# Recurrence of a hybrid encoder layer: filler in two runs per step, output one step later, x replaced in place

## The chip, the cores and the metric
One core of one Trainium2 chip. The metric is the device time of the whole kernel in microseconds, median of several runs. The engines are TensorE (PE, with its weight loads PEld), VectorE (DVE), ScalarE (ACT), GpSimd (POOL) and SyncE (SP); SP and POOL issue the DMAs of the part that matters here.

## What is computed
One encoder layer on a sequence of 2048 tokens of width 1024. A combined input projection feeds two mixers and two gates; this change touches the RWKV-7 mixer's delta-rule recurrence and the projection that runs beside it.
```
proj = x @ w_in                       # 43 columns of 128: hyena, rwkv, gates
def rwkv_step(S, inp):
    r, w, k, v, kk, a = inp
    sa = einsum('dbhvk,dbhk->dbhv', S, -kk)
    S = S * w[..., None, :] + sa[..., :, None] * (kk * a)[..., None, :] + v[..., :, None] * k[..., None, :]
    y = einsum('dbhvk,dbhk->dbhv', S, r)
    return S, y
_, ys = scan(rwkv_step, S0, xs)       # one scan per direction, then summed, normalized and gated
```
Behind it stand the hyena mixer's long convolutions by Fourier transform, the merge with the gates, and a SwiGLU feed-forward block.

## The kernel before
The program runs `project` (a part of the input projection and the recurrence's inputs), then `chain` (the recurrence), `hyena`, `merge` and `ffn`. The scan is done in chunks of 64 tokens: 32 chunks forward, then 32 backward, 64 steps (n = 0 to 63) in eight groups of eight. In `chain` the order on PE is written out by hand; the other engines' order is made by a scheduler from the program's order, priorities and its own times.

A step (`step(n)`, line 789) is three small products that hang on each other. **R** (tile pR, line 800) is the group's gram blocks G times the state and values in tile VS; ScalarE copies it (line 803). **S** (pS, line 808) applies the inverse X to that copy; ScalarE copies the result into tile SV (line 811). **D** (pD, line 816) is the state's update, which VectorE adds and scales into the next step's VS (lines 822, 823). The output **Y** (pY, lines 827 and 829) takes A, VS, SV and the masked gram Gr; in the backward half `normed` normalizes it on VectorE and ScalarE. All these products use part of the array (64 rows or columns); each is 8 calls, shown as 16 instructions.

Beside a step stands other work, `beside(n)`: **T**, the transposes pT of the next step's inputs (line 782); in steps 0 to 2 of a group three, three and two **grams** pG of the group that follows (line 677; rows ABp come by DMA into two buffers, VectorE masks the products, lines 656); in step 7 and the next group's step 0 the two halves of an **inverse** (`finish`, pW, lines 722 and 735). What `finish` needs is made by `invert`, issued after step 2: POOL moves the grams through DRAM (lines 696, 697), VectorE runs 62 small operations (lines 702, 704), transposes (line 709), and POOL stores (line 710). In the backward half there are also transposes pgt (line 865) and products pgg (line 897) of the output's gate. The PSUM tag "pg" has three buffers for all of these.

**Filler** is the rest of the input projection: 88 blocks of 128 columns by 512 tokens, each eight triples of passes (lines 202 to 204: hi by hi, lo by hi, hi by lo) over the whole array. `columns()` (line 908) yields a triple at a time. `order` goes through the four blocks of 512 tokens of x; one block lies on chip as xh and xl, so x is replaced three times. `share(n)` gives a step so much filler that filler and other work are even over the steps; in step 61 and after there is none.

`step` yields three times: after R, after S, and after D with Y. Each time `fill` gives a third of the filler and of the other work, in turns in proportion. Before a new x block `columns()` yields -14.0, and `hold` then keeps the filler back until steps of that cost have gone by:
```
def main():
    while True:
        t = next(more, None) if hold[0] <= 0 else None
        if t is None:
            return
        if t < 0:
            hold[0] = -t
            return
```
Of the kernel before, what the change touches and what calls it, by code (L numbers as in the profile page):

```python
# [9 lines left out]
F32 = mybir.dt.float32  # L10
# [6 lines left out]
P = 128  # L17
# [172 lines left out]
class Layer:  # L190
# [431 lines left out]
    def chain(self):  # L622
        tc, nc, i = self.tc, self.nc, self.i
        mm, tt, ts = nc.tensor.matmul, nc.vector.tensor_tensor, nc.vector.tensor_scalar
        NG, N = 8, 2 * NCH
        with tc.tile_pool(name="ch", bufs=1, reuse_waits="tile") as s, tc.tile_pool(name="chp", bufs=1, space=PSUM, reuse_waits="tile") as ps:
# [162 lines left out]
            def step(n):  # L789
# [3 lines left out]
                BK, SV = ins.pop(n)  # L793
                A = As[n % 2]
                VS = VSs.pop(n)
# [6 lines left out]
                with tc.high_priority(offset=AHEAD):  # L802
                    nc.scalar.copy(R, p)
                yield 0.33
                p = ps.tile([P, HP, 64], F32, name="pS", tag="pc", bufs=1)
# [3 lines left out]
                with tc.high_priority(offset=AHEAD):  # L809
                    for j in range(2):  # L810
                        nc.scalar.copy(SV[opp[j], j], p[opp[j]])
                yield 0.33
                pd = ps.tile([P, HP, 64], F32, name="pD", tag="pD", bufs=1)
# [3 lines left out]
                for j in range(2):  # L817
                    if (n + 1) % NCH == 0:
                        break
                    S1, q = VSs[n + 1][opp[j], j], opp[j]  # L820
                    with tc.high_priority(offset=AHEAD):
                        tt(out=S1, in0=pd[q], in1=VS[q, j], op=ALU.add)
                        tt(out=S1, in0=S1, in1=Dks[q, d, :, c:c + 1].broadcast_to([64, HP, 64]), op=ALU.mult)
                Y = ps.tile([P, HP, 64], F32, name="pY", tag="pY", bufs=1)
                for hp in range(HP):
# [8 lines left out]
                else:  # L834
                    normed(c, Y)
                yield 0.34

            out, ys = {}, {}

# [61 lines left out]

            xs = {2: self.x2}
            self.cut, self.rush, self.stores = 2, RUSH, nc.sync

            uh, gates = [*range(12)], [*range(27, NIN)]
            order = [(b, gates if b > 1 else uh + gates) for b in (2, 1, 3, 0)]

            def columns():
                seq = [(b, ct) for b, cts in order for ct in cts]
                nxt, raw = self.nxt  # L910
                for n, (b, ct) in enumerate(seq):
                    w = nxt
                    if n + 1 < len(seq):
                        nxt = self.parts(raw)
                    if b not in xs:
                        xs[b] = self.load_x(self.xp1, b, 1)
                    if n + 2 < len(seq):
                        raw = self.column(seq[n + 2][1])
                    if n and b != seq[n - 1][0]:
                        yield -14.0  # L920
                    yield from self.block(ct, b, *w, xs)

# [37 lines left out]

            hold = [0.0]

            def main():
                while True:
                    t = next(more, None) if hold[0] <= 0 else None
                    if t is None:
                        return
                    if t < 0:
                        hold[0] = -t
                        return  # L970
                    left[0] -= t
                    yield t


            def fill(need, aux, cost):
                d, a = main(), 0.0
                did = 0.0
                while did < need or a < cost:
# [14 lines left out]
                    else:  # L993
                        a += t

            with tc.manual_schedule(engines={mybir.EngineType.PE}):
                begin(0)
# [12 lines left out]
                near(0)  # L1010
                outward(0)
                self.fps = ps, "pg", 3
                taps, pieces = iter(()), [1, 2, 3]
                self.rush = 0
                for n in range(N):
                    g, st = divmod(n, NG)
                    if st == 0 and g + 1 < N // NG:
                        begin(g + 1)
                    cost, aux = beside(n)
                    sh = share(n)  # L1020
                    if n == LAST + 1:
                        taps = self.filt(0, 0)
                    if n >= LAST + 1:
                        aux.append(self.part(taps, 4.0))
                        cost += 4.0
                    if n + 1 < N:
                        outward(n + 1)
                    if n + 2 < N:
                        fetch(n + 2)
                    if n > NCH + 2 and n % 2 == 1:  # L1030
                        given(place(n - 2)[1])
                    for k in range(n + 1, N if n >= LAST else min(n + 2, N)):
                        if k not in VSs:
                            near(k)
                    if n == LAST:
                        self.open()
                    for need in step(n):
                        fill(sh * need, aux, cost * need)
                        hold[0] -= max((sh + cost) * need, 2.0)
                    fill(0.0, aux, 1e9)  # L1040
                    if n >= LAST and pieces:
                        self.taken(pieces.pop(0))
                    if st == len(GRAMS) - 1 and g + 1 < N // NG:
                        invert(g + 1)
                for part in (gated(2), channel_major(1), channel_major(0), gated(0)):
                    self.pull(part, 1e9)
                    self.pull(taps, 0.8)
# [633 lines left out]
```

## Time and profile before
| | us |
|---|---|
| median of 3 timed runs | 4077.75 (4075.48 to 4081.51) |
| the profiled execution | 4068.93 |
| its span in the profile | 4067.2 |
| from the first R to the R of step 61 | 875.1 |
| TensorE busy in these | 816.95 |

A row of time has the start, the duration, engine, line, operation, what is written and read, how many are merged, and in brackets the idle time before it with what ended it. Ends of products are modelled, so distances between starts tell what they take.

### The profile page before, as it was taken

The page shows a single profiled execution, that of the slowest core. Times are in us where ns is not written, and L with a number is a line of the kernel's source. Part 1 is how long each engine was busy: PE and PEld are TensorE (multiplying, and loading weights), DVE is VectorE, ACT ScalarE, POOL GpSimd, SP SyncE. Part 2 cuts the span into 40 slices and gives each one's busy share as a digit, 9 for nine tenths or more (in the row PEclk, how much of TensorE's full clock was granted, in tenths as well). Part 3 has the DMA queues.
Part 4 walks back from the last instruction along what each step waited for, and adds up shares of the span by engine and source line. Part 5 has one row for each costly group of instructions (what it writes and reads, how often), then busy time and mean ns, then how long its engine had stood idle before and what let it go on. Part 6 is the DMA issues. An engine that isn't in the chain of part 4 may idle for free. (4 is left out here: it accounts for less than half of the span.)

```text
span 4067.2 us, 64483 instructions
## 1 busy us (share of the span) xinstructions
PE 3870.1 (95%) x25872; PEld 3130.6 (77%) x25872; DVE 2421.1 (60%) x3823; ACT 1484.1 (36%) x2912; POOL 76.8 (2%) x107
## 2 busy tenths in 40 slices
PE   8999999899998999888898999999999999999998
PEld 6766557677776777788887899788888878888887
DVE  5456885556656666778877656544444465444444
ACT  3345662223335556756554323211111141111113
POOL 0000000000000000000000000000000000000000
PEclk9999999899898999899999999999999999999999
DMA  4556877666666766412224433411111133111111
GB/s 137 175 168 176 224 205 236 192 195 184 201 205 193 205 198 192 118 50 70 63 74 135 159 114 123 160 58 52 47 47 47 47 104 104 47 47 47 47 47 42
DMA packets 389186, 501.83 MB, mean 123 GB/s; under 512 B 134852, under 2 KB 270541, under 8 KB 388181
## 3 DMA queue, kind: packets, MB, share of 16 engines
q1 hardware_dynamic: 362775, 443.13, 36.3%
q10 hardware_dynamic: 20736, 37.80, 3.1%
q0 software_dynamic: 5376, 16.78, 1.5%
q8 instruction: 204, 3.34, 0.3%
q14 instruction: 95, 0.78, 0.1%
HBM read 352.74 MB, written 127.93 MB: 118 GB/s over the span
## 5 line engine op out<-in xcount | busy, mean ns | idle before, releaser
L202 PE MATMUL acc<-xh,wh 128*128 128x512 f32 x1376 | 606.4, 441 | 9.1 <-ACT xh L197 9.1
L203 PE MATMUL acc<-xl,wh 128*128 128x512 f32 x1376 | 551.9, 401 | 6.4 <-DVE xl L198 6.4
L204 PE MATMUL acc<-xh,wl 128*128 128x512 f32 x1376 | 551.0, 400 | 0.5 <-DVE wl L198 0.5
L1618 DVE TENSOR_TENSOR acc<-pd,acc 128x1024 f32<-128x1024 f32 x320 | 387.7, 1221 | 69.9 <-PE pd L204 64.2
L197 ACT CAST fwh<-raw 128x1024 fp32r<-128x1024 f32 x132 | 138.6, 1050 | 704.7 <-PE pg L203 487.9
L202 PEld LDWEIGHTS acc<-xh,wh 128*128 128x128 f32 x1376 | 262.3, 191 | 127.4 <-issue 46.9
L1646 DVE TENSOR_TENSOR h<-pu,sg 128x512 f32<-128x512 f32 x88 | 60.9, 692 | 493.1 <-PE pu L204 485.7
L204 PEld LDWEIGHTS acc<-xh,wl 128*128 128x128 f32 x1376 | 262.8, 191 | 63.9 <-DVE wl L198 1.0
L203 PEld LDWEIGHTS acc<-xl,wh 128*128 128x128 f32 x1376 | 264.5, 192 | 57.4 <-DVE xl L198 10.2
L198 DVE TENSOR_TENSOR wl<-wraw,wh 128x512 fp32r<-128x512 f32 (+1 forms) x217 | 170.3, 792 | 188.4 <-ACT wh L197 181.2
L202 PE MATMUL pd<-fwh,hh 128*128 128x512 f32 x704 | 276.1, 392 | 2.3 <-DVE acc L1616 1.9
L204 PE MATMUL pu<-fxh,fwl 128*128 128x512 f32 x704 | 277.8, 395 | 0.0
L204 PE MATMUL pg<-fxh,fwl 128*128 128x512 f32 x704 | 277.8, 395 | 0.0
L202 PE MATMUL pg<-fxh,fwh 128*128 128x512 f32 x704 | 276.7, 393 | 0.2 <-DVE fxl L1533 0.2
L203 PE MATMUL pg<-fxl,fwh 128*128 128x512 f32 x704 | 276.8, 393 | 0.0
L203 PE MATMUL pu<-fxl,fwh 128*128 128x512 f32 x704 | 276.4, 393 | 0.0
L202 PE MATMUL pu<-fxh,fwh 128*128 128x512 f32 x704 | 275.9, 392 | 0.4 <-ACT fxh L1532 0.4
L203 PE MATMUL pd<-fwl,hh 128*128 128x512 f32 x704 | 275.6, 391 | 0.0
L204 PE MATMUL pd<-fwh,hl 128*128 128x512 f32 x704 | 274.6, 390 | 0.0
L198 DVE TENSOR_TENSOR fwl<-raw,fwh 128x1024 fp32r<-128x1024 f32 x132 | 161.3, 1222 | 166.6 <-ACT fwh L197 162.6
L197 ACT CAST wh<-wraw 128x512 fp32r<-128x512 f32 (+1 forms) x217 | 151.1, 705 | 198.3 <-PE acc L203 182.0
L1187 DVE STREAM_TRANSPOSE V<-U 128x1024 f32<-128x1024 f32 x96 | 181.1, 1955 | 34.3 <-ACT U L1222 14.1
(299 smaller groups left out, 7617.1 us busy)
## 6 DMA issues: line engine op xcount, KB each, us to landing
wraw<-in_w_in SPq DMA_DIRECT2D x130, 512.0 KB
ABp<-ABd SPq DMA_DIRECT2D x64, 512.0 KB
raw<-in_fg SPq DMA_DIRECT2D x44, 512.0 KB
raw<-in_fu SPq DMA_DIRECT2D x44, 512.0 KB
raw<-in_fd SPq DMA_DIRECT2D x44, 512.0 KB
ud<-ev ACTq DMA_DIRECT2D x84, 256.0 KB
ABd<-AB SPq DMA_DIRECT2D x32, 512.0 KB
gated<-ev SPq DMA_DIRECT2D x64, 256.0 KB
```

The source lines that it names most:

```text
L197: nc.scalar.copy(hi, src)
L198: nc.vector.tensor_tensor(out=lo, in0=src, in1=hi.bitcast(F32), op=ALU.subtract)
L202: mm(ps, ah, bh, start=start, stop=False)
L203: mm(ps, ah, bl, start=False, stop=False)
L204: mm(ps, al, bh, start=False, stop=stop)
L1187: self.nc.vector.transpose(V[:, :, sl].rearrange("p j c -> p c j"), U[:, :, sl].rearrange("p n c -> p c n"))
L1618: tt(out=acc[t], in0=pf, in1=acc[t], op=ALU.add)
L1646: tt(out=h, in0=put, in1=sg, op=ALU.mult)
```

## The change
A step now yields four times, with two shares: one of filler, one of the other work. After R there is the output of the step before (`output`, taken from the list `late`), the loads for step n + 2 and 0.34 of the other work, with no filler; after S half of the filler and then 0.33 of the other work; after D the same. `runs` issues the filler of a place in one piece and the other work behind it. The load of A is issued in its own step and not one step ahead. The hold is gone: while the last column of an x block is computed, each quarter of x is loaded, cast and split into the same xh and xl as soon as the two triples that read it are issued. After step 60 what is left of the filler is issued.
```
--- before.py
+++ after.py
@@ -791,7 +791,6 @@
                 g, st = divmod(n, NG)
                 G, Gr, X = grp[g]["G"], grp[g]["Gr"][st], Xs[g % 2]
                 BK, SV = ins.pop(n)
-                A = As[n % 2]
                 VS = VSs.pop(n)
                 T2 = T2s.pop(n)
                 p = ps.tile([P, HP, 64], F32, name="pR", tag="pc", bufs=1)
@@ -801,7 +800,12 @@
                 R = s.tile([P, HP, 64], F32, name="R", tag="R", bufs=1)
                 with tc.high_priority(offset=AHEAD):
                     nc.scalar.copy(R, p)
-                yield 0.33
+
+                if late:
+                    output(*late.pop())
+                if n + 2 < N:
+                    fetch(n + 2)
+                yield 0.0, 0.34
                 p = ps.tile([P, HP, 64], F32, name="pS", tag="pc", bufs=1)
                 for hp in range(HP):
                     for j in range(2):
@@ -809,7 +813,8 @@
                 with tc.high_priority(offset=AHEAD):
                     for j in range(2):
                         nc.scalar.copy(SV[opp[j], j], p[opp[j]])
-                yield 0.33
+                late.append((n, VS, SV, Gr))
+                yield 0.5, 0.33
                 pd = ps.tile([P, HP, 64], F32, name="pD", tag="pD", bufs=1)
                 for hp in range(HP):
                     for j in range(2):
@@ -821,6 +826,11 @@
                     with tc.high_priority(offset=AHEAD):
                         tt(out=S1, in0=pd[q], in1=VS[q, j], op=ALU.add)
                         tt(out=S1, in0=S1, in1=Dks[q, d, :, c:c + 1].broadcast_to([64, HP, 64]), op=ALU.mult)
+                yield 0.5, 0.33
+
+            def output(n, VS, SV, Gr):
+                d, c = place(n)
+                A = As[n % 2]
                 Y = ps.tile([P, HP, 64], F32, name="pY", tag="pY", bufs=1)
                 for hp in range(HP):
                     for j in range(2):
@@ -833,9 +843,8 @@
                     nc.sync.dma_start(hv(self.Yd[c]), ye)
                 else:
                     normed(c, Y)
-                yield 0.34
-
-            out, ys = {}, {}
+
+            out, ys, late = {}, {}, []
 
 
             def normed(c, Y):
@@ -899,26 +908,33 @@
                 tt(out=yo, in0=p, in1=yo, op=ALU.mult)
                 nc.sync.dma_start(self.yrd[:, :, tl].rearrange("c p t -> p c t"), yo)
 
-            xs = {2: self.x2}
             self.cut, self.rush, self.stores = 2, RUSH, nc.sync
 
             uh, gates = [*range(12)], [*range(27, NIN)]
             order = [(b, gates if b > 1 else uh + gates) for b in (2, 1, 3, 0)]
 
+
+
             def columns():
                 seq = [(b, ct) for b, cts in order for ct in cts]
+                xh, xl = self.x2
                 nxt, raw = self.nxt
                 for n, (b, ct) in enumerate(seq):
                     w = nxt
                     if n + 1 < len(seq):
                         nxt = self.parts(raw)
-                    if b not in xs:
-                        xs[b] = self.load_x(self.xp1, b, 1)
-                    if n + 2 < len(seq):
+                    new = seq[n + 1][0] if n + 1 < len(seq) else b
+                    if n + 2 < len(seq) and new == b:
                         raw = self.column(seq[n + 2][1])
-                    if n and b != seq[n - 1][0]:
-                        yield -14.0
-                    yield from self.block(ct, b, *w, xs)
+                    for k, t in enumerate(self.block(ct, b, *w, {b: (xh, xl)})):
+                        yield t
+                        if k % 2 and new != b:
+                            raw = self.wp.tile([P, 2, 512], F32, name="xraw", tag="wraw", bufs=2)
+                            sl = slice(k - 1, k + 1)
+                            nc.sync.dma_start(raw, i["xT"][:, sl, 512 * new:512 * new + 512])
+                            self.split(xh[:, sl], xl[:, sl], raw)
+                    if n + 2 < len(seq) and new != b:
+                        raw = self.column(seq[n + 2][1])
 
             more, left = columns(), [5.16 * 88]
 
@@ -958,16 +974,8 @@
                         hi = lv
                 return max(lo - costs[n], 2.0)
 
-            hold = [0.0]
-
             def main():
-                while True:
-                    t = next(more, None) if hold[0] <= 0 else None
-                    if t is None:
-                        return
-                    if t < 0:
-                        hold[0] = -t
-                        return
+                for t in more:
                     left[0] -= t
                     yield t
 
@@ -993,6 +1001,25 @@
                     else:
                         a += t
 
+
+            owed = [0.0]
+
+            def runs(need, aux, cost):
+                owed[0] += need
+                while need and owed[0] > 0.3:
+                    t = next(more, None)
+                    if t is None:
+                        owed[0] = 0.0
+                        break
+                    left[0] -= t
+                    owed[0] -= t
+                while aux and cost > 0:
+                    t = next(aux[0], None)
+                    if t is None:
+                        aux.pop(0)
+                    else:
+                        cost -= t
+
             with tc.manual_schedule(engines={mybir.EngineType.PE}):
                 begin(0)
                 for st in range(2):
@@ -1008,7 +1035,6 @@
                 for j in range(2):
                     nc.sync.dma_start(Dks[opp[j]], self.Dk[row[j]])
                 near(0)
-                outward(0)
                 self.fps = ps, "pg", 3
                 taps, pieces = iter(()), [1, 2, 3]
                 self.rush = 0
@@ -1023,10 +1049,7 @@
                     if n >= LAST + 1:
                         aux.append(self.part(taps, 4.0))
                         cost += 4.0
-                    if n + 1 < N:
-                        outward(n + 1)
-                    if n + 2 < N:
-                        fetch(n + 2)
+                    outward(n)
                     if n > NCH + 2 and n % 2 == 1:
                         given(place(n - 2)[1])
                     for k in range(n + 1, N if n >= LAST else min(n + 2, N)):
@@ -1034,14 +1057,17 @@
                             near(k)
                     if n == LAST:
                         self.open()
-                    for need in step(n):
-                        fill(sh * need, aux, cost * need)
-                        hold[0] -= max((sh + cost) * need, 2.0)
-                    fill(0.0, aux, 1e9)
+                    for dense, other in step(n):
+                        runs(sh * dense, aux, cost * other)
+                    runs(0.0, aux, 1e9)
+                    if n == LAST - 1:
+                        for _ in more:
+                            pass
                     if n >= LAST and pieces:
                         self.taken(pieces.pop(0))
                     if st == len(GRAMS) - 1 and g + 1 < N // NG:
                         invert(g + 1)
+                output(*late.pop())
                 for part in (gated(2), channel_major(1), channel_major(0), gated(0)):
                     self.pull(part, 1e9)
                     self.pull(taps, 0.8)
```
Three places in the order of the engines show it. First PE in step 12, a light one: from R on, before and after (pR is R, pY is Y, pT the transposes, pS is S, acc the filler).
```order
L800 MATMUL pR<-VS,G_5531 64x64 x8
L202 MATMUL acc<-xh_5977,wh 128x512
L203 MATMUL acc<-xl_5978,wh 128x512
L204 MATMUL acc<-xh_5977,wl 128x512
L782 MATMUL pT<-k_c_ident,BK 128x128
L202 MATMUL acc<-xh_5977,wh 128x512
```
The same place in the changed kernel:
```order
L799 MATMUL pR<-VS,G_5529 64x64 x8
L837 MATMUL pY<-VS,A_4632 64x64 x2
L839 MATMUL pY<-SV,rg 64x64 x2
...
L782 MATMUL pT<-k_c_ident,BK 128x128 x2
L812 MATMUL pS<-R,X_4629 64x64 x8
L202 MATMUL acc<-xh_938,wh 128x512
```
Before, five triples and two transposes stand between R and S, five and two between S and D with Y, and five behind Y; now Y of step 11 and two transposes stand between R and S, six triples in one run behind S and six behind D.

Second PE in step 9, which has three grams (pG): from S to D, before and after.
```order
L808 MATMUL pS<-R,X_4629 64x64 x8
L202 MATMUL acc<-xh_5977,wh 128x512
L203 MATMUL acc<-xl_5978,wh 128x512
L204 MATMUL acc<-xh_5977,wl 128x512
L677 MATMUL pG<-ABp 128x128 x8
...
L677 MATMUL pG<-ABp 128x128 x8
L816 MATMUL pD<-SV,T_6869 64x64 x8
```
The same place in the changed kernel:
```order
L812 MATMUL pS<-R,X_4629 64x64 x8
L202 MATMUL acc<-xh_938,wh 128x512
L203 MATMUL acc<-xl_939,wh 128x512
L204 MATMUL acc<-xh_938,wl 128x512
...
L677 MATMUL pG<-ABp 128x128 x16
L821 MATMUL pD<-SV,T_6868 64x64 x8
```
The two grams had two triples between them and one ahead; now four triples stand ahead and the grams follow each other.

Third ScalarE at the first change of x (xh is the block's high part), after.
```order
L197 CAST wh<-wraw 128x512
L197 CAST xh_938<-xraw 128x1024 x3
L344 COPY ev<-acc 128x512
L802 COPY R<-pR 128x256
L842 COPY ye<-pY 128x256
L815 COPY SV<-pS 64x256 x2
L197 CAST xh_938<-xraw 128x1024
```
Three of the four casts into the block that is still in use stand ahead of R's copy of the step that follows, the fourth behind S's.

## Rows read from the trace of the kernel before

**Rows 1.** The head of the profile's page.
```profile
span 4067.2 us, 64483 instructions
```

**Rows 2.** Table of stretches: busy time (and instructions) of each engine, clock, DMA share, GB/s.
```profile
741.70:1616.80 875.10, 816.95 (x9774) 637.10 (x9773) 537.94 (x1325) 371.10 (x971) 58.56 (x82) 0.95 0.67 197
907.10:921.40 14.30, 14.30 (x132) 11.09 (x131) 4.60 (x11) 5.31 (x11) 0.58 (x1) 1.00 0.65 205
...
784.40:810.00 25.60, 22.74 (x215) 16.88 (x215) 13.39 (x29) 8.50 (x17) 0.58 (x1) 0.87 0.75 219
1065.50:1086.70 21.20, 17.91 (x315) 15.02 (x315) 15.51 (x31) 8.81 (x18) 4.84 (x7) 0.77 0.69 196
1263.20:1324.60 61.40, 42.95 (x561) 33.56 (x560) 46.98 (x122) 31.41 (x97) 4.84 (x7) 0.83 0.61 175
1268.00:1274.80 6.80, 5.87 (x98) 4.48 (x94) 6.54 (x17) 4.74 (x12) 0.00 (x0) 1.00 0.71 199
```

**Rows 3.** Instructions of PE in order of time, a light step (start, us, ...).
```profile
903.06 0.29 PE L827 MATMUL pY<-VS,A 128*64 128x64 f32 x4
...
904.10 0.50 PE L202 MATMUL acc<-xh,wh 128*128 128x512 f32 x1
...
906.77 0.40 PE L204 MATMUL acc<-xh,wl 128*128 128x512 f32 x1
907.10 0.69 PE L800 MATMUL pR<-VS,G 128*64 128x64 f32 x16
907.72 0.50 PE L202 MATMUL acc<-xh,wh 128*128 128x512 f32 x1
908.05 0.40 PE L203 MATMUL acc<-xl,wh 128*128 128x512 f32 x1
908.28 0.39 PE L204 MATMUL acc<-xh,wl 128*128 128x512 f32 x1
908.52 0.27 PE L782 MATMUL pT<-k_c_ident,BK 128*128 128x128 f32 x1
908.54 0.47 PE L202 MATMUL acc<-xh,wh 128*128 128x512 f32 x1
```

**Rows 4.** The same, a step with three grams.
```profile
863.12 2.17 PE L677 MATMUL pG<-ABp 64*128 64x128 f32 x16 [3.09 <-DMA ABp<-ABd]
...
867.66 0.63 PE L203 MATMUL acc<-xl,wh 128*128 128x512 f32 x1
868.08 0.63 PE L204 MATMUL acc<-xh,wl 128*128 128x512 f32 x1
```

**Rows 5.** The same, behind the third hold.
```profile
1307.85 0.28 PE L722 MATMUL pW<-XT,G 32*32 32x32 f32 x2 [12.20 <-DVE XT L709]
```

**Rows 6.** Instructions on the tile xraw: ns minimum/median/maximum, first and last start.
```profile
L197 ACT CAST xh<-xraw x12: 1032/1046/1053, 783.1 to 1286.0; 128x1024 fp32r<-128x1024 f32 x12
```

**Rows 7.** VectorE in order of time, masks of a gram.
```profile
900.35 0.42 DVE L656 TENSOR_TENSOR G<-pG,k_c_maskA 128x256 f32<-128x256 f32 x1 [2.77 <-PE pG L677]
```

**Rows 8.** PE in order of time, a gram right behind another.
```profile
1094.73 1.65 PE L677 MATMUL pG<-ABp 64*128 64x128 f32 x12 [3.70 <-DVE rg L656]
```

**Rows 9.** POOL's DMAs around two inversions, one of either half.
```profile
901.08 3.11 POOL L696 DMA_DIRECT2D Nd<-G  x4 [57.75 <-DVE G L656]
...
951.39 0.56 POOL L710 DMA_DIRECT2D Wd<-W  x1 [41.69 <-issue]
...
1489.03 3.11 POOL L696 DMA_DIRECT2D Nd<-G  x4 [52.79 <-DVE G L656]
...
1545.52 0.56 POOL L710 DMA_DIRECT2D Wd<-W  x1 [48.93 <-issue]
```

**Rows 10.** PE in order of time, the inverse's products behind the second of these.
```profile
1548.93 1.20 PE L722 MATMUL pW<-XT,G 32*32 32x32 f32 x62 [1.61 <-DVE vr L854]
```

**Rows 11.** ScalarE in order of time, light step.
```profile
907.89 0.37 ACT L803 COPY R<-pR 128x256 f32<-128x256 f32 x1 [3.30 <-PE pR L800]
910.70 0.62 ACT L197 CAST wh<-wraw 128x512 fp32r<-128x512 f32 x1 [2.44 <-PE acc L203]
```

## Prediction
> **What bounds the kernel now.** All times here are of the profiled execution: 4068.9 us, of which 4067.2 are its span [rows 1]. The timed runs have a median of 4077.75, 8.8 us more; I make the sum on the profile and take its difference off the median. I read the table of stretches first. The recurrence's 61 steps that have filler run from 741.7 to 1616.8 us, and in these 875.1 us TensorE is busy for 816.95 [rows 2]. So TensorE binds, and there are two kinds of loss to look for: time in which its products cost more than they need to, and the 58 us of idleness, with the lowered clock (mean 0.95) that goes with them. DMA engines are busy for 0.67 of the stretch, VectorE for 537.94 us, ScalarE for 371.10; none is full, but each can be late.
>
> Second, the order of instructions in time of a light step, with no gram or inverse in it [rows 3]. I read starts, since a product's printed end is modelled. A projection pass follows the one before after 0.23 (908.05 to 908.28). When a product on part of the array follows, 0.33 passes (906.77 to 907.10): +0.10. The last of the small products is followed by a projection pass later by some 0.10 than by one of its own kind, and the pass after that comes 0.33 later instead of 0.23 (907.72 to 908.05): +0.10 again. A transpose set among passes costs no such thing: it starts 0.24 after its neighbour and the next pass 0.02 after it, and what it takes is the 0.11 that it takes anywhere. So a step's filler is dear where it is cut up by small products and free where transposes cut it.
>
> A projection triple (hi*hi, lo*hi, hi*lo) is thus 3 x 0.233 = 0.70. The light step of 14.30 us has 15 triples, 10.5, and nothing idle [rows 2]: 3.3 are its own products and four transposes, 0.5 the switches. With these three numbers I rebuild any step from its count of triples, and what its length has beyond that is loss.
>
> **The change, part by part.** *Two runs instead of pieces.* By the order of PE, in the 61 steps: small products follow whole-array work 238 times now and 188 after; the way back 239 and 189; passes that start behind small products 226 and 122. At 0.10 each that is 5.0 + 5.0 + 10.4 saved. Small products of one kind behind those of another grow from 22 to 62, taken at 0.1 each too: -4. Sum **-16 us**. The 601 triples and all small products stay; only their order changes.
>
> *The hold goes.* At each of three changes of the x block the kernel now gives no filler for some steps. Steps 3 and 4 take 25.60 us for 15 triples; rebuilt, 14.3 + 3.3 = 17.6. Steps 22 and 23 take 21.20 for 6 triples and one half of an inverse (2.0): rebuilt 13.3. Steps 36 to 39 take 61.40 for 24 triples: 16.8 + 4 x 3.3 + 2.0 + 3.1 (other small products, switches) = 35.1. The losses are 8.0, 7.9 and 26.3 [rows 2]; the largest piece is 12.20 of waiting for the inverse's transposes, since steps without filler ran ahead of VectorE [rows 5]. In these stretches the clock is 0.87, 0.77 and 0.83. All of it comes from the hold: **-42**.
>
> *The swap in place.* In exchange, each quarter of x is loaded into the buffer that the last column's passes have just left. Cast and subtract must wait for these passes, the next column needs the quarter six triples later, and on SP and ScalarE other work stands behind them. The casts take 1.05 each [rows 6]. Nothing in the trace shows such a swap; the nearest is another load that is asked for only when its buffer is free: the third gram's rows, for which PE waits 3.09 [rows 4]. Ends: nothing, or 3.1 for each of 12 quarters, 37. I take one such wait in each of three swaps, **+9**; six triples and the step between them (some 10 us) mostly cover a load.
>
> *Grams in pairs.* The rows of the third gram in a step are still asked for behind the first; the runs leave about the time between them that the pieces did, so that wait stays. New is that 16 times two grams stand back to back (3 now): four PSUM tiles out of three, so the second waits for masks of the first. Two masks are 0.42 each [rows 7]; the dearest case now is 3.70 [rows 8]. Ends 0 and 13 x 3.7 = 48. I take 0.9 for each, half of it beside the wait for rows that comes anyway: **+6**.
>
> *The inverse.* Five steps after a group's last grams, PE needs what POOL and VectorE have made of them. From the first DMA to the store of the inverse it is 50.3 us in the first half (901.08 to 951.39) and 56.5 in the second (1489.03 to 1545.52), where VectorE also normalizes; the products can start some 3.4 later (1548.93, with 1.61 of waiting left) [rows 9, 10]. So about 54 and 60 us. A light step after has 12 triples: 8.4 + 3.3 + 0.4 = 12.1, in the second half 11.7 to 12.3 by turns; four of them, the rest of the gram's step (3 to 4.5) and the way to the inverse's products (2.2) are 55 us in the first half and 54 in the second. The first half just holds. The second is late by 6 in three groups, 18, and a clock that falls behind such a wait costs 2 more each; 6 us of it are there already. **+18**; ends 0 and the rival below.
>
> *S behind R.* No filler stands between R and S any more; the step before's output does, 1.0 us (903.06 to 904.10) [rows 3], and two or more transposes. R's copy starts 0.8 after R and takes 0.37 [rows 11]; S comes 1.9 after R's start at the earliest, against 1.2 to 1.3. The cover is 0.6, one cast on ScalarE (0.62) in the way uses it up. Ends 0 and 61 x 0.6 = 37; I take **+3**, as R's copy is issued with priority. D and the next R keep a run of mostly four to seven triples ahead of them, 2.8 us or more (one to three and grams in the heavy steps), where pieces covered the same copies and updates before: nothing. A is now loaded in the step in which it was needed before and used one step later: nothing. The end of the loop has no filler either way; its output moves behind R there too: nothing.
>
> Sum: -16 - 42 + 9 + 6 + 18 + 3 = **-22 us**: 4047 on the profile, **4056** on the median.
>
> **The rivals.** *The new waits don't come* (pairs, inverse and S hidden): 4077.75 - 16 - 42 + 9 = 4029. For it: VectorE is busy for only 61% of the stretch. Against it: in the second half PE waits for the inverse already [rows 10].
>
> *The swap waits as long as the hold did*: 37 instead of 9, 4084. For it: the three swaps meet the grams' rows on SP's one queue in two of three cases. Against it: the ten us of cover.
>
> *The inverse becomes the bound in all seven groups*, on the slower side: the same VectorE work squeezed into shorter steps stretches the chain to 60 us in the first four groups as well. Each then waits 6 and loses 2.5 to the clock, 34 more: 4090. It decides where the chain passes 55 us; 54 is close to it. Against it: the first-half chain is 50.3 with steps of 12.9 to 14.3 us.
>
> *The clock falls in the stretches without projection passes*: R, Y, transposes and S now stand together for 2.5 us or more in each step. If the run behind S stood at half rate in every third step, 18 passes at 0.42 (867.66 to 868.08) instead of 0.23 [rows 4] are 3.4, 20 times 69: 4125. Against it: from 1268.0 to 1274.8 PE had no projection pass at all, transposes among its products, 5.87 of 6.80 busy, and the granted clock was 1.00 [rows 2]; it fell behind stretches with real waiting. The Trainium skill speaks for this rival (TensorE: Matmul & The Clock Gate, "PE-mode transpose": transposes don't count as a busy TensorE in the same way; "Why this matters for your kernels": keep the engine continuously busy). The trace does not agree for stretches of this kind, and the row decides; by the page alone the sum would come out on the slower side.
>
> **How the numbers follow.** Forecast 0.52 (own range 4040 to 4072), no new waits 0.18, swap 0.11, inverse everywhere 0.11, clock 0.08. From 4024 to 4092 all but the clock's case and some edges lie inside. What a measurement can tell here is 0.2%, 8.2 us. Below 4069.6 lie most of the forecast and the first rival, 0.66; within 0.2% some of forecast, swap and inverse, 0.15; above, 0.19.
>
> **What would show it.** In the profile after: light steps of 12.1 us with two runs; no idle stretch of 12 us around the third swap; waits for the inverse's transposes of 5 to 7 us in the last three groups and none in the first; waits of S for R's copy below 5 us in all; 842 to 860 us from the first R to the 62nd. It is wrong if that stretch is over 875, and wrong in its reasons if it is short and the inverse never waits, or if the clock in light steps is below 1.00.

## The result, and the profile after

The changed kernel took 4041.41 us in the median of 4 runs (4037.57 to 4047.38), the kernel before 4079.63 beside it: 0.9905 of it, 95% interval [0.9883, 0.9926], 38 us less. On another chip, in the first experiment, it was 0.9934 [0.9911, 0.9956], 27 us by the ratio and 25 by the medians. The forecast was 22 less; 4041.41 lies inside its range of 4040 to 4072, 1.4 us from the lower end. Profile against profile it is 21.6 us (4068.93 and 4047.38), but that it comes so close to 22 says little: the profile of before is shorter than the three timed runs it was shown with, that of after is the longest of its four.

The head of the page of after, and its table of stretches (as [rows 2]): from the first R to the R of step 61; a light step; step 3 with the first swap; steps 36 to 38 with the third; steps 39, 47 and 55 with the inverse.
```profile
span 4045.6 us, 64349 instructions
```
```profile
748.45:1600.03 851.58, 796.92 (x9742) 645.43 (x9742) 534.90 (x1322) 373.31 (x972) 58.55 (x82) 0.96 0.69 202
910.22:922.40 12.18, 12.18 (x121) 9.67 (x121) 7.10 (x19) 5.21 (x11) 0.00 (x0) 1.00 0.59 168
788.16:803.88 15.72, 12.76 (x121) 9.52 (x121) 7.10 (x10) 8.11 (x14) 0.58 (x1) 1.00 0.91 277
1234.33:1275.43 41.10, 38.68 (x375) 31.61 (x374) 35.60 (x94) 27.11 (x76) 0.00 (x0) 0.96 0.71 211
1275.43:1299.66 24.23, 15.33 (x243) 12.43 (x242) 14.64 (x36) 8.48 (x26) 4.84 (x7) 0.79 0.61 167
1401.14:1421.58 20.44, 15.91 (x242) 12.84 (x241) 10.67 (x24) 8.02 (x24) 4.83 (x7) 0.83 0.65 182
1518.40:1537.82 19.42, 14.63 (x239) 11.85 (x238) 10.71 (x26) 7.92 (x24) 3.72 (x5) 0.82 0.63 170
```
The 61 steps went from 875.1 to 851.6 us: 20.0 less of busy TensorE, 3.5 less of idleness (58.2 to 54.7). The light step is full, at clock 1.00, with 12 triples in 12.18 us. What is left stands in few places: step 39 alone has 8.9 us idle and a clock of 0.79.

The light step in order of time (as [rows 3]): R, the output of the step before, two transposes, S, the first run.
```profile
910.22 0.69 PE L799 MATMUL pR<-VS,G 128*64 128x64 f32 x16
910.73 0.29 PE L837 MATMUL pY<-VS,A 128*64 128x64 f32 x4
...
911.76 0.44 PE L782 MATMUL pT<-k_c_ident,BK 128*128 128x128 f32 x2
912.13 0.68 PE L812 MATMUL pS<-R,X 64*64 64x64 f32 x16
912.74 0.50 PE L202 MATMUL acc<-xh,wh 128*128 128x512 f32 x1
913.08 0.40 PE L203 MATMUL acc<-xl,wh 128*128 128x512 f32 x1
913.31 0.40 PE L204 MATMUL acc<-xh,wl 128*128 128x512 f32 x1
```
S starts 1.91 after R without a wait; the first pass of the run costs 0.34, the next 0.23.

The waits of PE in that stretch, after (what it waited for, us in all, times, longest):
```profile
PE pG L677 <- DMA ABp<-ABd: 17.4, 10, 3.6
PE pW L722 <- DVE XT L709: 15.0, 4, 7.4
PE pG L677 <- DVE rg L656: 6.9, 9, 1.3
PE pG L677 <- DVE wl L198: 4.4, 2, 2.3
PE pW L722 <- DVE vr L863: 3.2, 2, 1.6
PE acc L203 <- DVE xl L198: 3.2, 2, 2.4
PE pG L677 <- ACT T L786: 1.9, 1, 1.9
PE pS L812 <- ACT R L802: 1.6, 1, 1.6
```
The grams' rows (17.4) and the inverse (15.0, and 3.2 that the profile puts down to vr) make 35.6 of some 54 us. S waited for R's copy once.

To place the rest, I priced every step's products with the prediction's numbers (a pass 0.233, a transpose 0.11, 0.10 for each kind of change) and took the price from the step's length. In light steps the two agree to 0.2 us (0.9 where the second half's products pgg stand among them). What a step has beyond its price is called loss: idle time and half clock together, and what the prices leave out. Steps 0 to 59, us, one profiled execution each:

| kernel | products | loss: steps with grams | 3, 4, 22, 23, 26, 27, 36 to 38 | 39 | 47, 55, 56 | other | sum |
|---|---|---|---|---|---|---|---|
| before | 752.8 | 58.5 | 25.4 | 16.7 | 8.7 | 3.9 | 866.0 |
| after | 731.6 | 61.4 | 10.2 | 11.8 | 16.7 | 7.2 | 839.0 |
| after, second profile | 731.6 | 55.2 | 8.1 | 12.9 | 16.5 | 7.2 | 831.5 |
| two runs alone | 729.6 | 59.2 | 22.1 | 12.4 | 10.1 | 10.2 | 843.5 |
| swap alone | 757.6 | 55.0 | 9.1 | 2.0 | 26.7 | 8.3 | 858.6 |
| swap, evened | 736.1 | 72.5 | 10.2 | 8.4 | 18.9 | 9.7 | 855.9 |
| after + inverse later | 731.6 | 59.4 | 9.7 | 9.3 | 6.2 | 6.9 | 823.0 |
| after + three row buffers | 731.6 | 35.1 | 11.1 | 12.5 | 17.0 | 7.4 | 814.8 |
| after + both | 731.6 | 30.1 | 8.2 | 8.8 | 6.6 | 8.0 | 793.2 |
| two runs, hold + both | 729.6 | 37.2 | 19.9 | 14.6 | 4.4 | 8.2 | 814.0 |

Of the 21.2 us of products that the change saves, 3.5 are five triples that now stand in step 60, which is longer by as much. The two profiles of after differ by 7.5 us in these steps, 6.2 of it in the steps with grams: so much a single execution can be off there. In the other columns differences of 3 us or less tell nothing.

### The profile page after: what moved, and what is told of

Read it like the earlier page. It is cut to its first block, busy times and chain, and to the rows that moved or that the text cites. A ratio compares the mean times of both kernels' runs of the same rounds, so it can differ in the third digit from the quotient of the medians.

```text
span 4045.6 us, 64349 instructions
## 1 busy us (share of the span) xinstructions
PE 3847.6 (95%) x25872; PEld 3135.6 (78%) x25872; DVE 2418.9 (60%) x3823; ACT 1489.7 (37%) x2914; POOL 76.8 (2%) x107
## 5 line engine op out<-in xcount | busy, mean ns | idle before, releaser
L202 PE MATMUL acc<-xh,wh 128*128 128x512 f32 x1376 | 584.9, 425 | 9.2 <-ACT xh L197 9.2
L1213 DVE STREAM_TRANSPOSE V<-U 128x1024 f32<-128x1024 f32 x96 | 181.2, 1955 | 30.3 <-ACT U L1291 12.4
```

The source lines that it names most:

```text
L202: mm(ps, ah, bh, start=start, stop=False)
L1213: self.nc.vector.transpose(V[:, :, sl].rearrange("p j c -> p c j"), U[:, :, sl].rearrange("p n c -> p c n"))
```

## The experiments

The theory on trial was the forecast's terms given to their edits: two runs -16 and the new waits (pairs, inverse, S) +27 to the one half, swap for hold -33 to the other. The rivals put the gain or the waits on the other half. Ratios are to the kernel before on the same chip; its median was 4065 to 4074 us there. Distances from the changed kernel "by the ratios" take its 0.9934 of the first experiment. Taken from the 0.9905 of the first measurement, a gain over the changed kernel would come out 12 us smaller; so the stretch from the first R to the R of step 61 (851.6 and 844.1 us in the two profiles of after) is given beside the main ones.

**The change again, and its two halves.**

> The changed kernel once more, unaltered, on the chip of the next three runs. Its profiled execution was 21.5 us below that of before, the medians are 38 us apart. Theory: the 16 us between the two are chance of two single executions, so a second profile shows the same stretch (first R to R of step 61, 851.6 us) within 8 us and the same three waits for the inverse's transposes (7.4, 2.9 and 3.2 us), and the median stays 34 to 42 below before. Rival: the profile's distance is the true one, then the median comes out 18 to 26 below.

Measured: 4041.32, 0.9934 [0.9911, 0.9956]. The stretch is 844.1 us; the waits for XT are 16.0 in all. The stretch came again within 8 us and the same three waits with it, but the median is 25 below before (27 by the ratio): in the rival's span or just above it, not in the theory's. The intervals of the two chips overlap from 0.9911 to 0.9926.

Two runs with the old hold: `columns` and `hold` as before, `runs` takes its filler through `main`.
```
-                    t = next(more, None)
+                    t = next(main(), None)
...
+                        hold[0] -= max(sh * dense + cost * other, 2.0)
```


> Two runs and late output, but the old hold and the old load of a whole x block. Theory (the forecast's terms hold and add up: products -16, pairs, inverse and S +27, and the hold's 42 us stay): 0 to 12 us slower than before. Rival 1 (rebuilt from the trace after: products 18 to 21 less, grams +4, inverse +8 as the third inverse falls into the hold anyway): 5 to 12 us faster. Rival 2 (the 16 us by which the medians beat the forecast come from the runs): 20 to 30 us faster.

Measured: 4045.48, 0.9951 [0.9932, 0.997], 20 us faster, where the theory had 0 to 12 slower and the first rival 5 to 12 faster; the second rival's time fits. The new waits don't belong to this half. In the table the products are 23 lower (4 of it six triples that went behind step 59) and the losses unchanged: the inverse's 10.1 in steps 47 to 56 hardly above the 8.7 of before.

The swap in place, with three pieces and the output in its own step:
```
-            xs = {2: self.x2}
...
-                        hold[0] -= max((sh + cost) * need, 2.0)
```


> Only the change of x in place, without a hold; three pieces of filler and the output in its own step as before. Theory (hold 42 less, one wait of 3 us in each swap): 33 us faster than before, and no wait over 4 us in steps 3, 4, 22 to 25 and 36 to 39. Rival 1 (filler that is no longer held back only moves: the inverse and the grams' rows wait as long): 10 us faster or less. Rival 2 (the swap costs nothing): 42 us faster.

Measured: 4067.99, 1.0005 [0.9987, 1.0023]: nothing. Its waits of PE, in the same stretch:
```profile
PE pG L677 <- DMA ABp<-ABd: 26.0, 11, 3.7
PE pW L722 <- DVE XT L709: 16.7, 5, 8.1
```
and step 55:
```profile
1545.99 0.28 PE L722 MATMUL pW<-XT,G 32*32 32x32 f32 x2 [8.12 <-DVE XT L709]
```
The hold's steps lose 16 less and step 39 15 less, but steps 47, 55 and 56 lose 18 more. Filler that was held back had made the later steps longer: the four steps ahead of step 47 now have 47.2 us together and those ahead of step 55 45.5 (before 52.7 and 50.0). The inverse's chain did not shrink with them (57.4 and 56.2 us from POOL's first DMA to the store, before 56.4 and 56.5), and it is waited for there. So the first rival, filler that only moves, has the time.

**What a cut of the filler costs.** The output's products cut into four parts:
```
+                    if hp < 3 and n < 60:
+                        t = next(more)
+                        left[0] -= t
+                        owed[0] -= t
```


> The changed kernel with the output's products cut into four parts by three triples of filler, taken from the run behind S, so that 60 steps have three more changes from filler to small products and back. Theory (each change costs 0.10 on the way out, 0.10 on the way back and 0.10 on the first pass, as read from the light step): 177 times 0.3 to 0.33 are 53 to 58 us more than the changed kernel. Rival (the starts in the trace show these prices, but the products pay only part of them, and the gain of the two runs comes from elsewhere): 25 us more or less.

Measured: 4115.07, 1.0132 [1.011, 1.0153], 81 us above the changed kernel by the ratios. The light step is 13.19 instead of 12.18 us with the same products; in order of time:
```profile
931.76 0.50 PE L202 MATMUL acc<-xh,wh 128*128 128x512 f32 x1
932.10 0.39 PE L203 MATMUL acc<-xl,wh 128*128 128x512 f32 x1
932.33 0.40 PE L204 MATMUL acc<-xh,wl 128*128 128x512 f32 x1
932.65 0.34 PE L837 MATMUL pY<-VS,A 128*64 128x64 f32 x4
932.82 0.29 PE L839 MATMUL pY<-SV,rg 128*64 128x64 f32 x4
933.03 0.51 PE L202 MATMUL acc<-xh,wh 128*128 128x512 f32 x1
```
1.01 us for three cuts, 0.34 each, is the price read before. The trace has 180 such cuts (the expectation reckoned 177), 61 us. So the price holds, but the total is above the theory's 53 to 58: of the 20 that remain 12 are longer waits for the grams' rows, 29.5 us in place of 17.6.

**The inverse later.** In step 7 of a group its first products go from between R and S to behind the first run:
```
-                yield 0.0, 0.34
+                yield 0.0, 0.34 if st < NG - 1 else 0.12
```


> The changed kernel with one number altered: in step 7 of a group the inverse's first products stand behind the first run of filler (four triples more, some 3 to 4 us later) and not between R and S. Theory (the inverse is what the changed kernel still waits for): the waits for its transposes fall from 7.4, 2.9 and 3.2 us to about 4, 0 and 0, and with the second products' waits and the lowered clock behind them 10 to 16 us go: 10 to 16 below the changed kernel's time. Rival 1 (they only hide another wait: the next group's first R waits for rows of G that are loaded behind these products): each of seven steps waits 2 us more there, and the time is the same or up to 10 us longer. Rival 2 (run-to-run changes are as large as this): no difference over 4 us.

Measured: 4018.79, 0.9893 [0.9869, 0.9917]; 17 us below the changed kernel by the ratios, 22 by the medians of the same chip, a little more than the theory's 10 to 16. The profiled execution is the slowest of its six (4039.84), so its rows show the gain in the steps and not in the total; its stretch is 835.6. Steps 39, 47 and 55 in the table of stretches:
```profile
1271.25:1293.00 21.75, 16.26 (x243) 13.09 (x242) 14.87 (x36) 8.54 (x26) 4.84 (x7) 0.76 0.64 185
1392.30:1406.38 14.08, 12.93 (x242) 10.41 (x241) 10.77 (x24) 8.12 (x24) 4.83 (x7) 1.00 0.80 225
1506.51:1521.65 15.14, 13.73 (x239) 10.99 (x238) 10.97 (x26) 7.92 (x24) 3.73 (x5) 0.89 0.74 205
```
Step 47 fell from 20.44 to 14.08 us and has its clock back. The waits for XT are 3.9 and 1.6 now, both in step 39; the rival's rows of G cost 1.5 us in all, in two waits.

The same cure on the swap alone (`yield 0.6` ahead of the first half's products):

> The kernel before with x changed in place and no hold, as in the run of the swap alone, which came out at 1.0005 of before; now the inverse's first products stand one piece later in step 7 (between S and D). Theory (the 26 us that the hold cost in its own steps were given back at the inverse, since filler that was held back made the later steps longer and covered it): the waits for the inverse's transposes, 16.7 us in the swap's profile, fall below 6, and the time is 12 to 20 us below before. Rival (the swap itself gives back what the hold cost): the inverse's waits fall, but 5 us or less go.

Measured: 4055.47, 0.9981 [0.9971, 0.9992], 8 us below before. That lies between theory and rival: a piece moves the products by 2.2 us only (from 2.0 to 4.2 us behind R in step 55), and the waits for XT fell from 16.7 to 11.4, not below 6.

The swap with what a piece gives too much taken off the next:
```
-                did = 0.0
+                did = over[0]
...
+                over[0] = did - need if on else 0.0
```


> The kernel before with x changed in place and no hold (alone: 1.0005 of before), where what a piece of filler gives too much is taken off the next one, so that steps no longer shrink towards the end (light steps there fell from 14.3 to 10.3 us; now 12 to 13 triples in all of them); filler cut up as before, the output in its own step. Fewer triples stand singly too, which by the prices of the light step is 15 us of products. Theory (the swap's gain was given back because the last groups' short steps no longer cover the inverse): the losses of steps 47 and 55, 10.4 and 13.2 us in the swap's profile, fall by 10 or more together, and 20 to 30 us go against the swap alone. Rival (evenness does nothing for the inverse, only the switches count): those losses stay, and 15 us go or less.

Measured: 4069.61, 0.9994 [0.9981, 1.0007]: no gain over the swap alone. The theory misses; the rival's time fits, its reason only in part. The products fell as reckoned, 21.5 with eight triples moved behind step 59; steps 47, 55 and 56 lost 7.8 less; but step 39 lost 6.4 more and the steps with grams 17.5 more. Why the grams cost more there was not tried.

**The grams.** Three buffers for their rows:
```
-                AB = s.tile([P, HP, 256], F32, name="ABp", tag="ABp", bufs=2)
+                AB = s.tile([P, HP, 256], F32, name="ABp", tag="ABp", bufs=3)
```
with rows asked for three grams ahead, BK in two buffers and w1 in one.

> The changed kernel with three buffers for the grams' rows ABp where there were two, each asked for one gram earlier; to make room, the step's input BK has two buffers (it is read one step after its load only) and w1 one. In the changed kernel's two profiles PE waits 17.4 and 17.6 us for these rows, ten times, and steps with grams are 50 to 60 us longer than their products, the lowered clock behind the waits included. Theory (the rows are late because they are asked for late): the ten waits fall below 3 us together and 15 to 30 us go against the changed kernel. Rival 1 (the queue or the DMA engines are full there, so an earlier request lands no earlier): waits of 12 us or more stay, 5 us or less go. Rival 2 (the grams then run into the masks of the gram before: three PSUM tiles): the waits for rg grow from 7 to over 14 us, and 8 us or less go.

Measured: 4022.33, 0.9898 [0.9882, 0.9914], 15 us below the changed kernel by the ratios, 17 to 24 in the stretch. Its stretch and waits:
```profile
747.95:1575.39 827.44, 783.37 (x9743) 633.99 (x9742) 534.27 (x1322) 373.34 (x972) 58.56 (x82) 0.98 0.70 208
PE pW L722 <- DVE XT L709: 15.0, 4, 7.3
PE pG L677 <- DVE rg L656: 13.0, 16, 1.9
```
No wait for ABp is left; that for masks of a gram before grew from 6.9 to 13.0, so the second rival is in it too, but the steps with grams lose 35 instead of 55 to 61, more than the waits that went: the clock had fallen behind them, and its mean in the stretch is 0.98 for 0.96.

A place of its own for each gram in nine steps:
```
-                yield 0.92
+                yield 1.14
```


> The changed kernel, but in the steps with two or three grams behind the first step of a group each gram has a place of its own (between R and S, behind the run of S, behind the run of D), where two stood back to back. Theory (back to back, the second gram waits for masks of the first and for its rows): these nine steps lose 24 us in the changed kernel's profile and 10 in that of before, so 8 to 14 us go. Rival 1 (the forecast's 6 us for pairs): 3 to 8. Rival 2 (the last gram of a group comes later, by 1 to 4 us in two groups, and the inverse waits as much more): the waits for the inverse's transposes grow by 3 to 8 us in the groups that end in steps 47 and 55, and nothing is won.

Measured: 4033.69, 0.9923 [0.9907, 0.9939], not told apart from the changed kernel. The last rival holds: the steps with grams lost 17 us less than in the second profile of after, the waits for XT rose from 16.0 to 24.2, and most of what the grams gave is lost again.

**Together.** Both cures in the changed kernel:

> The changed kernel with the inverse's first products behind the first run of filler in step 7 and three buffers for the grams' rows: the edits of the two runs before in one kernel. Each alone was some 18 us below the changed kernel. Theory (two separate waits): the gains add to 30 to 40 us, 3985 to 4005 us where the kernel before takes 4065, and PE waits below 3 us for ABp and below 8 for the inverse's transposes. Rival (both fill the same slack: shorter steps with grams leave the inverse's chain less time): the inverse's waits come back to 10 us or more, and 15 to 25 us go against the changed kernel.

Measured: 4006.23, 0.9842 [0.9821, 0.9863], the fastest; they add up (37 us by the ratios, 38 to 46 in the stretch). No wait for ABp is left, and that for XT is below 8, as the theory says:
```profile
746.30:1552.12 805.82, 774.38 (x9742) 627.16 (x9742) 534.43 (x1322) 373.89 (x972) 58.72 (x82) 0.99 0.72 213
PE pG L677 <- DVE rg L656: 13.0, 16, 1.9
PE pW L722 <- DVE XT L709: 5.6, 2, 3.9
```
With the grams apart as well and three quarters of step 7's filler ahead of the inverse:

> The same with two more edits: in step 7 three quarters of the filler stand ahead of the inverse's first products and one quarter behind D, and the grams have places of their own. Theory (what is left behind the two edits is the inverse in the second half, 9 us at step 39, and the masks of grams that stand back to back, 13 us of waits): another 5 to 15 us below the kernel with the two edits. Rival (the last gram comes later and D, the second products and the next R stand closer together in step 7): no more than 4 us either way, with waits for rows of G or for w in place of those for XT.

Measured: 4020.05, 0.9879 [0.9857, 0.9901], 15 us worse by the ratios, outside theory and rival. Its waits show what took the place:
```profile
PE pW L722 <- DVE XT L709: 8.8, 6, 1.8
PE pR L799 <- DMA G<-ABd: 8.5, 4, 3.3
```
The next group's R waits for rows of G, whose load the program issues only behind the inverse's first products; the rival named this wait. At last the hold beside both cures:

> The two runs and late output with the old hold and load of x, and on top the two edits that took waits away from the changed kernel (inverse's first products behind the first run of filler in step 7, three buffers for the grams' rows). It differs from the fastest kernel so far (0.9842 of before) in the hold and the load alone. Theory (the hold costs time, but without it shorter steps ran into the inverse and the grams' rows and gave the gain back; with both cured the gain shows): 15 to 30 us slower than that kernel, 0.988 to 0.992 of before. Rival (the hold is worth no more than the change showed between the two kernels with runs, some 7 us, cured or not): 0.984 to 0.987.

Measured: 4027.94, 0.9888 [0.9861, 0.9915]. That is 19 us above the kernel without a hold by the ratios, in the theory's span; the intervals touch at their ends. What the hold costs shows once the waits that swallow it are gone; the two kernels ran on two chips, each beside its own before.

## Why the prediction was right, and what its terms did not say

In its sum it holds, and so do most of its terms; one loss was given to the wrong cause. From the first R to the R of step 61 the change saves 23.5 us in the first profile: 17.7 of products and 5.8 of losses, where the forecast had 16 and 6 (31.0 in the second, 17.7 and 13.3). Of these, before the first R 6.7 are given back and behind step 61 4.8 gained; neither was forecast, nor tried.

*Two runs, -16:* 17.7, the half alone gained 20, and each cut costs 0.34 in the light step. Yet a light step itself gains next to nothing: without its triples at 0.70 it has 3.80 us before (14.30 with 15) and 3.78 after (12.18 with 12). One cut is saved there, but the transposes that stood free among passes now stand among small products, where two of them take 0.37 us (911.76 to 912.13) for 0.11 each. Priced by the distances of starts, some 12 of the 18 us stand in the steps with grams, which had cut the filler most. (Changes from one small product to another are 92 before and 124 after by the trace, 32 more; the forecast had 40 more.)

*The hold, -42, and the inverse, +18 over 6.* The losses of the hold's steps and step 39, 25.4 and 16.7, make the 42. What stands there now is 10.2 for the swaps (forecast 9; steps 3 and 36 to 38 alone 3.6 and 6.1, of which the price misses 1.8 at the products pgg) and 11.8 for the inverse at step 39; steps 47, 55 and 56 lose 8.0 more than before. So the inverse has 19.8 of new loss, for 18, spread otherwise than the even three that the forecast had, and the groups of the first half hold (0.5 or less each), as reckoned. At step 39 the filler that kept PE from running ahead [rows 5] did not spare it the wait, after:
```profile
1276.98 0.66 PE L782 MATMUL pT<-k_c_ident,BK 128*128 128x128 f32 x4
1284.98 0.28 PE L722 MATMUL pW<-XT,G 32*32 32x32 f32 x2 [7.35 <-DVE XT L709]
1286.82 1.91 PE L722 MATMUL pW<-XT,G 32*32 32x32 f32 x62 [1.55 <-DVE XT L709]
...
1291.15 0.63 PE L202 MATMUL acc<-xh,wh 128*128 128x512 f32 x1
1291.58 0.63 PE L203 MATMUL acc<-xl,wh 128*128 128x512 f32 x1
```
The passes at the end are at half rate, 0.43 apart. The chain is longest here: from POOL's first DMA to the store (as [rows 9]),
```profile
1218.20 3.11 POOL L696 DMA_DIRECT2D Nd<-G  x4 [48.12 <-DVE G L656]
...
1283.46 0.56 POOL L710 DMA_DIRECT2D Wd<-W  x1 [55.01 <-issue]
```
65 us, where the other groups of the second half have 56 and 57 and those of the first 49 to 55. In this stretch and in that of the group for step 55 VectorE is busy for
```profile
1218.20:1283.50 65.30, 57.01 (x564) 46.26 (x563) 51.76 (x143) 41.04 (x118) 3.72 (x6) 0.96 0.77 224
1465.30:1522.30 57.00, 55.31 (x564) 44.95 (x564) 45.70 (x134) 43.13 (x118) 3.69 (x6) 1.00 0.65 191
```
51.76 and 45.70 us; four subtractions of the new x, 1.22 each, are most of the difference.

*What the terms did not say* is whose they are. Add up what steps 39, 47, 55 and 56 lose: 25.4 us before, 28.5 after, 22.5 with the runs alone, 28.7 with the swap alone. PE's waits for XT in the stretch are 14.9, 15.0, 12.0 and 16.7 in the same order. It is much the same sum in all four, and mainly its place changes: before, one wait made nearly all of it.
```profile
PE pG L677 <- DMA ABp<-ABd: 20.6, 11, 3.1
PE pW L722 <- DVE XT L709: 14.9, 3, 12.2
PE pG L677 <- DVE rg L656: 3.9, 2, 3.7
```
The words "all of it comes from the hold: -42" were therefore wrong for 16.7 of it: the hold had shown the inverse's wait at step 39, and taking it away moves that wait to the steps that become short. Since the same forecast booked the inverse's wait anew, the sum was right. That the two entries belong together was not seen, so it was luck that both stood in one change. Given to the two edits, the same terms failed: 20 faster where they say 11 slower, and nothing where they say 33 faster. What the hold really was worth, some 16 us in its own steps, came out as some 19 when the other waits were gone.

*Pairs, +6:* 2.9 more in the first profile, 3.3 less in the second. The waits for masks grew (3.9 to 6.9), those for rows fell (20.6 to 17.4). All waits in front of grams, with those that the profile puts down to wl and to T, were 25.9 us before and 30.6 and 27.5 after, so the 6 is near. It is not what pairs cost: with the grams apart these waits are 16.8 and the steps lose 17 less. *S behind R, +3:* one wait of 1.61, at the first swap, where the order of ScalarE had casts of x ahead of R's copy.

*The rivals.* "The new waits don't come" gave 4029; the first median lies midway between it and the forecast, but the waits are there. The swap did not wait as long as the hold had (10.2 of loss for 37), and no group of the first half waits for its inverse. The clock's case fell: light steps stand at 1.00 with R, output, transposes and S together for 2.5 us, and each of the twelve falls of the clock in the stretch stands in or just behind a wait of PE of 1.3 us or more (0.79 in step 39). By the Trainium skill (TensorE: Matmul & The Clock Gate, "PE-mode transpose") transposes do not count as a busy TensorE in the same way; no row here shows a lower clock for it.

*What would show it* came as listed but for the size of the waits: 12.18 us a light step (12.1), no idle stretch of 12 us, 851.6 from the first R to the 62nd (842 to 860), S's waits 1.6 in all (below 5). The waits for the inverse are 7.35, 2.92 and 3.17, each with some 1.6 behind it, where 5 to 7 were said.

Not settled: why the medians gain 25 to 38 us and the stretch 23.5 to 31. The one piece shown is the scatter in the steps with grams.

## What to carry to other kernels

When a loss contains a wait for a chain on other engines that does not get shorter with the steps (49 to 65 us here), do not book that wait to the edit that starves the engine: it moves to whichever steps become short, so price an edit by the wait that ends next. Terms of a sum that fits may still belong to other edits than one thinks, which only runs of the halves show; here curing two waits (rows asked for late, an inverse wanted early) was worth about as much as the change itself and brought 0.9842. And cut long filler as seldom as possible: each cut by products on part of the array cost 0.34 us. But look what comes to stand between the small products instead: in the light step it took the gain back.

## What had not been expected

A wait of a few us costs more than itself: with three row buffers all waits in front of grams fell from 30.6 and 27.5 to 15.3 us, by 15 and 12, and the steps with grams lost 26 and 20 less; with both cures the mean clock of the stretch is 0.99 where it was 0.96. And cures added up, but more of one was not better: beside the row buffers, moving the inverse's products behind four to five triples gave 4006 us, behind six to seven with the grams apart 4020, since another load waits for the same products (two edits at once, so what each did is not shown).
